# A two-layer decoder trunk on one core: 166 instead of 168 tokens through the first layer's dense experts, and the second layer's mixing tables loaded in that mixing

## The chip, the cores and the metric

The kernel runs on one core of a Trainium2 chip (trn2). The metric is the device time of one execution in microseconds (us); smaller is better. Several executions were timed, and one more was profiled.

## The reference, cut to what matters

Two layers are applied to 256 tokens of 1024 channels. Each layer mixes tokens and then channels:

```python
def hybrid_layer(x, ...):
    h = rms_norm(x, norm1_g) * (1 + sc1) + sh1
    q, k, v, cb, cc, ch, su, sv = split(h @ w_in)
    y_attn = sliding_window_attention(q, k, v, attn_sink, rel_bias)   # needs the bias table
    y_conv = short_conv_mixer(cb, cc, ch, conv_w)
    y_sgu  = chunked_spatial_gating(su, sv, sgu_w, sgu_b)             # needs the gating weights
    x = x + g1 * (concat(rms_norm of the three) @ w_out)
    h2 = rms_norm(x, norm2_g) * (1 + sc2) + sh2
    return x + g2 * peer_ffn(h2, ...)

def peer_ffn(h, w_pq, sub_keys, expert_down, expert_up):
    # per token: 8 heads x 16 experts out of 16384, found by product keys
    act = gelu(einsum('td,thkd->thk', h, expert_down[experts]))
    return einsum('thk,thkd->td', gate * act, expert_up[experts])
```

`expert_down` and `expert_up` have 16384 rows of 1024 floats each in every layer.

## The kernel before

**Stages.** For each of the two layers the program runs `mixing` (attention, convolution and gating, then `w_out`), `retrieval` (which experts each token wants, and with which gate) and `experts`. The last is split into a **down half** (128 steps, one for each group of 128 rows of `expert_down`) and an **up half** (`combine`, 128 steps over `expert_up`).

**Two ways through the experts.** The first `T = DENSE[layer]` tokens go the dense way: TensorE multiplies them with all 16384 experts, 8 matrix products of 128 x 128 by 128 x T for each step in either half, and a gate that is zero for unwanted experts selects. The activations, 128 steps x T columns, lie in the large buffer `arena` (in `acts`); step i of the up half reads the i-th T columns, which are then free. The other `TS = 256 - T` tokens go by rows. They are put in sets of n = 64, 32, 16 or 8 tokens (`token_sets`). For a set of n tokens, each gather (an indirect DMA by POOL, in `fetch`) brings 128 rows of 1024 floats, one to each partition, so that a set takes n gathers from `down_rows` and n from `up_rows`. VectorE (DVE) multiplies a gathered tile with the tokens and sums (`dot`, the down half), or adds it, weighted, to the set's sum (`add_row`, the up half). TensorE adds the set's sum into the result with eight small products, the folds (`fold_set`): `early_folds` puts one behind each of eight steps, starting 8 steps after the set's last row was added; the last set's folds stand in step 127 (`folds`). There are 88 such tokens in the first layer (64 + 16 + 8) and 96 in the second (64 + 32).

**What sets the order.** The engines run their queues in order. The dense weights are streamed in five buffers of 1 MB (`raw`), issued by SP and by ScalarE (ACT) when TensorE has freed one. Gathers are issued by POOL when a buffer for them is free; the buffers are parts of `spots` (the space of `hh`) and of `arena` that are unused just then. Within `experts` and around its ends the program's order is written by hand (`tc.manual_schedule()`, opened by `manual.enter_context` and ended by `manual.close()`). Outside, the order of an engine's queue is chosen at build time by a scheduler that places an instruction where it believes it to be ready.

**The tables.** The mixing needs a bias table (`R_BIAS`, 1 MB), gating weights (`R_SW`, 256 KB) and their offsets (`R_SB`, 128 KB), at columns 45 to 56 x 256 of `arena`. `R_SW` is masked in place by an AFFINE_SELECT on POOL, and two columns of `R_Z` are zeroed. For the second layer the loads are issued on SP's queue in the first layer's up half, in step `56 * S // T + 4`, and the mask follows on POOL in step 124 (`tables_rest`).

Of the kernel before, what the change touches and what calls it, by code (L numbers as in the profile page):

```python
# [18 lines left out]
DEPTH = 2  # L19
S = 256  # L20
DC = 8
# [22 lines left out]
DENSE = (168, 160)  # L44
# [31 lines left out]
def token_sets(n):  # L76

    out, off = [], 0
    for m in (64, 32, 16, 8):
        if n & m:  # L80
            out.append((off, m))
            off += m
    assert off == n and len(out) <= 3
    return out
# [3 lines left out]
def hybrid_trunk(ctx: ExitStack, tc: tile.TileContext, x_in, c_in, vec_in, w_ada, w_first, w_in, w_out, w_pq,  # L88
                 keys, down, down_rows, up, up_rows, rel_bias, sgu_w, sgu_b, out):
    nc = tc.nc  # L90
# [61 lines left out]
    R_HF = region(104 * S, DC, S)  # L152
# [9 lines left out]
    R_BIAS = region(45 * S, 8, S)  # L162
# [404 lines left out]
    def tables(layer, after=None):  # L567
        if after is not None:
            for r in (R_BIAS, R_SW, R_SB):
                nc.scalar.copy(r[:, 0, 0:1], after)  # L570
        q = nc.gpsimd if layer == 0 else nc.sync
        q.dma_start(R_BIAS, rel_bias)
        q.dma_start(R_SW, sgu_w[layer])
        q.dma_start(R_SB, sgu_b[layer])
        return lambda: tables_rest(layer)

    def tables_rest(layer):
        nc.gpsimd.affine_select(R_SW, R_SW, pattern=[[0, 4], [1, P]], compare_op=OP.is_ge, fill=0.0,
                                base=0, channel_multiplier=-1)
        nc.gpsimd.memset(R_Z[:, :, 0:2], 0.0)  # L580
        qg = work.tile([P, 1], F32, name="qg", tag="qg", bufs=1)
        nc.vector.tensor_scalar(qg, vec[:, layer, V_QG:V_QG + 1], 0.125, None, op0=OP.mult)
        return qg
# [8 lines left out]
    def mixing(layer, qg, update=None, late=None):  # L592
# [245 lines left out]
        if layer == 0:  # L838
# [3 lines left out]
            qg = tables(0, R_HF[:, DC - 1, 0:1])()  # L842
            for n, ps in enumerate(pss):
                evac(n, ps)
        else:
# [5 lines left out]
            manual.close()  # L851
            evac(1, ps)
# [202 lines left out]
    def experts(layer, rest):  # L1055
# [4 lines left out]
        NG = T // 4  # L1060
# [5 lines left out]
        R_DROW = spots[:, 3, :]  # L1066
        beyond = [region(at * S, D) for at in (80, 84) if at * S >= P * T]
        passing = []
# [122 lines left out]
        def gate_use(g, ps, done):  # L1191
            v = ps.rearrange("p (t i) -> p i t", t=4)
            a = acts[:, :, 4 * g:4 * g + 4]
# [25 lines left out]
        def combine(layer, late, dotted):  # L1219
# [28 lines left out]
            for i in range(128):  # L1248
# [30 lines left out]
                if i == 56 * S // T + 4 and layer + 1 < DEPTH:  # L1279
                    others = tables(layer + 1)  # L1280
                if i == 124 and layer + 1 < DEPTH:
                    qg = others()
# [18 lines left out]
        for i in range(128):  # L1301
# [8 lines left out]
            if j == 1:  # L1310
                tdone = 4 * gdone
                pend.append((pair, gelu(pair, ps, tdone), tdone))
                if len(pend) > 1:
                    act_use(*pend.popleft())
# [203 lines left out]
```

## Time and profile before

| | us |
|---|---|
| three timed runs | 1544.82, 1545.63 (median), 1546.74 |
| the profiled execution | 1544.97 |
| its span, first to last instruction | 1543.3 |

The table below adds up the busy time of three engines in each stage of the profiled execution, with the share of time in which the 16 DMA engines moved something (by overlapping packets it can pass 1) and what they moved. TensorE's busy time is modelled and counts overlapping products once.

| stage, us from the start | TensorE | VectorE | POOL | DMA share | GB/s |
|---|---|---|---|---|---|
| layer 0 mixing, 0 to 129 | 122.02 | 99.12 | 5.66 | 0.97 | 379 |
| retrieval, 129 to 188 | 58.04 | 48.83 | 5.05 | 0.49 | 171 |
| down half, 188 to 502 | 313.43 | 242.72 | 123.21 | 1.01 | 399 |
| up half, 502 to 800 | 298.00 | 136.80 | 113.46 | 1.01 | 416 |
| layer 1 mixing, 800 to 897 | 96.92 | 64.42 | 0.61 | 0.52 | 174 |
| retrieval, 897 to 955 | 57.04 | 47.84 | 5.06 | 0.49 | 173 |
| down half, 955 to 1255 | 299.27 | 231.75 | 124.94 | 1.00 | 397 |
| up half, 1255 to 1543 | 282.95 | 128.76 | 125.18 | 0.97 | 405 |

### The profile page before, as it was taken

The numbers are of one execution on the slowest core, as the hardware profiler recorded it, in microseconds if no ns is written. First come the engines' busy times: TensorE is split into PE (matmuls) and PEld (weight loads), VectorE is DVE, ScalarE is ACT, GpSimd is POOL, SyncE is SP. The second block draws the span as 40 slices with busy tenths as digits, with TensorE's granted clock in tenths as the row PEclk, the third lists the DMA queues.
The fourth block names the chain that finished last, engine by engine and source line by source line (L and its number), as shares of the span: only waits on it lengthen the run. The fifth ranks groups of instructions, "written<-read, shape, count | busy, mean of one in ns | idle before, by whom it ended". The sixth has DMA issues, their size and how long they took to land.

```text
span 1543.3 us, 28519 instructions
## 1 busy us (share of the span) xinstructions
PE 1527.7 (99%) x11244; PEld 1494.3 (97%) x11244; DVE 1000.2 (65%) x2249; ACT 478.7 (31%) x1380; POOL 503.2 (33%) x424
## 2 busy tenths in 40 slices
PE   8999999999999999999999999999999999999998
PEld 6879999999999999999999899999999999999998
DVE  7787879677687544444467578797777764443435
ACT  2256322466564000000036663234656620000000
POOL 0000125344334433443300002154344444444542
PEclk9999999999999999999999999999999999999999
DMA  9998299999999999999985573999999999999996
GB/s 387 386 362 319 93 312 380 422 422 422 422 422 420 420 422 423 422 424 423 422 319 169 170 257 107 280 409 423 421 423 423 422 422 423 423 423 423 424 422 283
DMA packets 122120, 570.65 MB, mean 370 GB/s; under 512 B 14292, under 2 KB 14820, under 8 KB 89986
## 3 DMA queue, kind: packets, MB, share of 16 engines
q1 hardware_dynamic: 48818, 240.54, 39.7%
q0 software_dynamic: 55744, 202.36, 32.6%
q10 hardware_dynamic: 17424, 125.93, 19.7%
q8 instruction: 88, 1.44, 0.3%
q14 instruction: 46, 0.38, 0.1%
HBM read 563.50 MB, written 4.09 MB: 368 GB/s over the span
## 4 chain that ended last, share of the span: by engine, by line
PE 84%; DMA 10%; DVE 3%; issue 1%; ACT 1%; POOL 0%; DVEq 0%; ACTq 0%; SPq 0%; POOLq 0%
PE acc L1225 37%; PE ch L403 28%; DMA arena<-in_down_rows,arena 5%; DMA spots<-in_down_rows,arena 3%; PE ch L405 2%; PE ch L406 2%; PE ch L407 2%; PE g L1187 2%; PE ch L494 1%; DVE raw L256 1%; PE g L999 1%; PE acc L405 1%; PE acc L407 1%; PE acc L406 1%; DMA raw<-in_w_ada 1%
## 5 line engine op out<-in xcount | busy, mean ns | idle before, releaser
L1225 PE MATMUL acc<-arena,raw 128*128 128x168 f32 (+1 forms) x4096 | 577.0, 303 | 0.0
L1225 PEld LDWEIGHTS acc<-arena,raw 128*128 128x128 f32 x4096 | 570.8, 190 | 0.0
L403 PE MATMUL ch<-arena,raw 128*128 128x168 f32 (+2 forms) x3808 | 564.3, 307 | 0.6 <-issue 0.6
L403 PEld LDWEIGHTS ch<-arena,raw 128*128 128x128 f32 x3808 | 539.3, 190 | 7.6 <-issue 3.9
L1153 DVE SCALAR_TENSOR_TENSOR spots<-arena,spots 128x1024 f32<-128x1024 f32 x154 | 197.8, 1285 | 263.3 <-DMA arena<-in_up_rows,arena 262.0
L1128 POOL DMA_INDIRECT arena<-in_up_rows,arena x159 | 216.6, 1362 | 283.8 <-DMA arena<-in_up_rows,arena 196.8
L1128 POOL DMA_INDIRECT arena<-in_down_rows,arena x147 | 177.0, 1204 | 223.3 <-DVE arena L1138 177.2
L1138 DVE SCALAR_TENSOR_TENSOR arena<-arena,spots 128x1024 f32<-128x1024 f32 x147 | 177.6, 1220 | 47.8 <-DMA arena<-in_down_rows,arena 46.0
L1171 ACT ACTIVATE arena<-arena,parts 128x128 f16<-128x128 f16 x164 | 64.6, 394 | 107.2 <-DVE arena L1161 85.1
L434 ACT ACT_TABLE_LOAD x6 | 7.7, 1283 | 247.9 <-PE acc L1225 247.8
L405 PE MATMUL ch<-hh,hi 128*128 128x256 f32 x288 | 82.6, 289 | 2.0 <-DVE arena L525 1.9
L406 PE MATMUL ch<-hh,lo 128*128 128x256 f32 x288 | 81.8, 284 | 0.0
L407 PE MATMUL ch<-hh,hi 128*128 128x256 f32 x288 | 81.8, 284 | 0.0
L1204 ACT ACTIVATE arena<-ch 128x336 f32<-128x336 f32 (+32 forms) x122 | 42.1, 346 | 123.7 <-PE ch L403 109.5
L1197 DVE SCALAR_TENSOR_TENSOR arena<-arena,g 128x336 f32<-128x336 f32 (+30 forms) x82 | 40.3, 492 | 49.6 <-ACT arena L1195 47.8
L256 DVE SCALAR_TENSOR_TENSOR raw<-raw,arena 128x1024 f32<-128x1024 f32 x48 | 58.4, 1221 | 12.2 <-DMA raw<-in_w_ada 12.1
L1128 POOL DMA_INDIRECT spots<-in_down_rows,arena x37 | 42.1, 1138 | 73.2 <-DVE spots L1138 54.7
L309 DVE TENSOR_TENSOR lo<-raw,hi 128x1024 fp32r<-128x1024 f32 x42 | 51.1, 1224 | 22.1 <-ACT hi L316 19.2
L1175 ACT ACTIVATE arena<-arena,parts 128x128 f16<-128x128 f16 x164 | 63.4, 387 | 0.0
L1173 ACT ACTIVATE arena<-arena,parts 128x128 f16<-128x128 f16 x164 | 63.4, 386 | 0.0
L1177 ACT ACTIVATE arena<-arena,parts 128x128 f16<-128x128 f16 x164 | 63.4, 386 | 0.0
L403 PE MATMUL ch<-arena 128*128 128x168 f32 (+1 forms) x448 | 63.0, 303 | 0.0
(239 smaller groups left out, 1754.9 us busy)
## 6 DMA issues: line engine op xcount, KB each, us to landing
raw<-in_up SPq DMA_DIRECT2D x64, 1024.0 KB
raw<-in_up ACTq DMA_DIRECT2D x64, 1024.0 KB
raw<-in_down SPq DMA_DIRECT2D x58, 1024.0 KB
raw<-in_down ACTq DMA_DIRECT2D x56, 1024.0 KB
raw<-in_w_ada SPq DMA_DIRECT2D x48, 512.0 KB
aside<-in_w_ada SPq DMA_DIRECT2D x48, 512.0 KB
raw<-in_w_pq SPq DMA_DIRECT2D x32, 512.0 KB
arena<-in_down SPq DMA_DIRECT2D x28, 512.0 KB
```

Of the source, the lines that this page charges most:

```text
L256: nc.vector.scalar_tensor_tensor(raw, raw, 1.0, cact, op0=OP.mult, op1=OP.mult, accum_out=mods[layer][:, col:col + 1])
L403: nc.tensor.matmul(dst, hi[:, cols], k[0], start=start, stop=stop, **kw)
L405: nc.tensor.matmul(dst, hi[:, cols], k[0], start=start, stop=False, **kw)
L406: nc.tensor.matmul(dst, lo[:, cols], k[0], start=False, stop=False, **kw)
L407: nc.tensor.matmul(dst, hi[:, cols], k[1], start=False, stop=stop, **kw)
L1128: nc.gpsimd.indirect_dma_start(out=held[n], out_offset=None, in_=rows if n >= TS else down_rows[:, :], in_offset=bass.IndirectOffsetOnAxis ...
L1138: nc.vector.scalar_tensor_tensor(row, row, 1.0, R_DX[which(k)[0]], op0=OP.mult, op1=OP.mult, accum_out=R_DOTS[:, k:k + 1])
L1153: nc.vector.scalar_tensor_tensor(R_SUM[s], row, w, R_SUM[s], op0=OP.mult, op1=OP.add)
L1171: nc.scalar.activation(og[0][:, 0, i, :], oh[:, 0, i, :], AF.Copy, scale=parts[:, 0, t + i:t + i + 1])
L1173: nc.scalar.activation(og[1][:, 0, i, :], oh[:, 0, i, :], AF.Copy, scale=parts[:, 1, t + i:t + i + 1])
L1175: nc.scalar.activation(og[0][:, 1, i, :], oh[:, 1, i, :], AF.Copy, scale=parts[:, 0, t + 2 + i:t + 3 + i])
L1225: nc.tensor.matmul(acc[d // 2][:, (d % 2) * S:(d % 2) * S + T], u[:, d * P:(d + 1) * P], acts[:, i, :], start=i == 0 and d % 2 == 0, stop= ...
```

## The change

The first layer's dense width goes from 168 to 166 tokens. Its rows part grows from 88 to 90 tokens in four sets: 64, 2, 16 and 8. The fourth of the four tiles of `spots` becomes the new set's, and the scratch `R_DROW`, which later serves as a gather buffer, moves to a part of `arena` that was a gather buffer of its own. The gate's one-hot products still run in groups of four tokens; of the last group only two columns are used. The tables of the second layer are now asked for in its own mixing, behind `manual.close()`, on POOL's queue; only the small `qg` product stays in step 124.

```diff
-DENSE = (168, 160)
+DENSE = (166, 160)
...
 def token_sets(n):
-    out, off = [], 0
-    for m in (64, 32, 16, 8):
-        if n & m:
-            out.append((off, m))
-            off += m
-    assert off == n and len(out) <= 3
-    return out
+    sizes = [m for m in (64, 32, 16, 8) if n & m]
+    if n & 2:
+        sizes.insert(1, 2)
+    assert sum(sizes) == n and len(sizes) <= 4
+    return [(sum(sizes[:k]), m) for k, m in enumerate(sizes)]
...
-        q = nc.gpsimd if layer == 0 else nc.sync
-        q.dma_start(R_BIAS, rel_bias)
-        q.dma_start(R_SW, sgu_w[layer])
-        q.dma_start(R_SB, sgu_b[layer])
-        return lambda: tables_rest(layer)
-
-    def tables_rest(layer):
+        nc.gpsimd.dma_start(R_BIAS, rel_bias)
+        nc.gpsimd.dma_start(R_SW, sgu_w[layer])
+        nc.gpsimd.dma_start(R_SB, sgu_b[layer])
         nc.gpsimd.affine_select(R_SW, R_SW, pattern=[[0, 4], [1, P]], compare_op=OP.is_ge, fill=0.0,
                                 base=0, channel_multiplier=-1)
         nc.gpsimd.memset(R_Z[:, :, 0:2], 0.0)
+
+    def q_gain(layer):
         qg = work.tile([P, 1], F32, name="qg", tag="qg", bufs=1)
...
             second_pair(ps)
             first_q(*outputs())
             manual.close()
+            tables(layer)
             evac(1, ps)
...
-        NG = T // 4
+        NG = -(-T // 4)
...
-        R_DROW = spots[:, 3, :]
         beyond = [region(at * S, D) for at in (80, 84) if at * S >= P * T]
+        R_DROW = spots[:, 3, :] if len(SETS) < 4 else beyond.pop()
...
-                if i == 56 * S // T + 4 and layer + 1 < DEPTH:
-                    others = tables(layer + 1)
                 if i == 124 and layer + 1 < DEPTH:
-                    qg = others()
+                    qg = q_gain(layer + 1)
```

Three places show how the instructions stand now. The first is POOL's queue at the end of the first layer's up half and the start of the second layer; `in_up_rows` are gathers (one line is a run of equal ones), `in_keys` belongs to the second layer's mixing. Before:

```order
L1128 DMA arena<-in_up_rows,arena 128x1024 x9
L1128 DMA spots<-in_up_rows,arena 128x1024
L1128 DMA arena<-in_up_rows,arena 128x1024 x2
L578 AFFINE_SELECT arena<-arena 128x512
L580 MEMSET arena 128x2x2
L865 DMA arena<-in_keys 128x2048
```

The same stretch of POOL's queue in the changed kernel, from the first gather of the up half on:

```order
L1126 DMA arena<-in_up_rows,arena 128x1024 x42
L574 MEMSET arena 128x2x2
L1126 DMA arena<-in_up_rows,arena 128x1024 x33
L569 DMA arena<-in_rel_bias 128x2048
L1126 DMA arena<-in_up_rows,arena 128x1024 x3
L570 DMA arena<-in_sgu_w 128x512
L571 DMA arena<-in_sgu_b 128x256
L572 AFFINE_SELECT arena<-arena 128x512
L1126 DMA arena<-in_up_rows,arena 128x1024 x12
L863 DMA arena<-in_keys 128x2048
```

The scheduler has moved the loads, the mask and the MEMSET up, out of the second layer's mixing and in among the first layer's gathers: the three loads stand behind 75 and 78 of the 90 gathers, and 12 gathers stand behind the AFFINE_SELECT, which reads what the load of `in_sgu_w` brings.

The second place is SP's queue in the first layer's up half. Before, the three loads stood between a load for the second layer's modulation (`aside`) and the dense weights (`raw`):

```order
L240 DMA raw<-in_up 128x2048
L242 DMA aside<-in_w_ada 128x1024
L572 DMA arena<-in_rel_bias 128x2048
L573 DMA arena<-in_sgu_w 128x512
L574 DMA arena<-in_sgu_b 128x256
L240 DMA raw<-in_up 128x2048 x3
L1278 DMA arena<-x_dram 128x2048
```

In the changed kernel they are gone from it:

```order
L240 DMA aside<-in_w_ada 128x1024
L238 DMA raw<-in_up 128x2048
L240 DMA aside<-in_w_ada 128x1024
L238 DMA raw<-in_up 128x2048 x3
L1277 DMA arena<-x_dram 128x2048
```

Nothing else moved on SP. The third place is TensorE's queue in the up half, where the folds of the first sets stand. Before, behind 784 products (98 steps):

```order
L1225 MATMUL acc<-arena,raw 128x168 x784
L1233 MATMUL acc<-fold_102,spots 128x64
L1225 MATMUL acc<-arena,raw 128x168 x8
L1233 MATMUL acc<-fold_102,spots 128x64
L1225 MATMUL acc<-arena,raw 128x168 x8
```

In the changed kernel the folds of the set of 64 begin a step earlier, and those of the set of 2 stand beside them:

```order
L1224 MATMUL acc<-arena,raw 128x166 x776
L1232 MATMUL acc<-fold_102,spots 128x64
L1224 MATMUL acc<-arena,raw 128x166 x8
L1232 MATMUL acc<-fold_102,spots 128x64
L1224 MATMUL acc<-arena,raw 128x166 x8
L1232 MATMUL acc<-fold_102,spots 128x64
L1232 MATMUL acc<-fold_102,spots 128x2
```

A fold waits for its set's last row, and the dense products behind it in TensorE's queue wait with it.

More of the change, by code (lines that the diff above doesn't have):

```diff
@@ L841, in mixing @@
             first_chunks(pss, first_norm())
-            qg = tables(0, R_HF[:, DC - 1, 0:1])()
+            tables(0, R_HF[:, DC - 1, 0:1])
+            qg = q_gain(0)
             for n, ps in enumerate(pss):
@@ L1192, in gate_use @@
             v = ps.rearrange("p (t i) -> p i t", t=4)
-            a = acts[:, :, 4 * g:4 * g + 4]
+            a = acts[:, :, 4 * g:min(4 * g + 4, T)]
+            v = v[:, :, :min(4, T - 4 * g)]
             if done < 128:
@@ L1310, in experts @@
             if j == 1:
-                tdone = 4 * gdone
+                tdone = min(4 * gdone, T)
                 pend.append((pair, gelu(pair, ps, tdone), tdone))
```

## The prediction, made before the changed kernel was run

> **What bounds the kernel now.** First the page's head and slices: a single core, whose granted TensorE clock shows no throttle, and a DMA row that stands at 9 wherever the experts run.
>
> ```profile
> span 1543.3 us, 28519 instructions
> PEclk9999999999999999999999999999999999999999
> DMA  9998299999999999999985573999999999999996
> GB/s 387 386 362 319 93 312 380 422 422 422 422 422 420 420 422 423 422 424 423 422 319 169 170 257 107 280 409 423 421 423 423 422 422 423 423 423 423 424 422 283
> ```
>
> The change works in the first layer's experts, so the stage windows come next: the down half once it has started up, and the up half.
>
> ```profile
> 255.00:502.00 247.00, 247.00 (x1920) 245.12 (x1920) 185.34 (x357) 136.09 (x473) 97.93 (x80) 1.00 1.02 422
> 502.00:796.00 294.00, 294.00 (x2073) 294.00 (x2072) 133.50 (x130) 4.80 (x9) 113.46 (x84) 1.00 1.01 419
> ```
>
> The columns are the stretch's length, then TensorE's products and weight loads, VectorE, ACT and POOL, the clock, the DMA share and GB/s. TensorE never idles in either half; the 16 DMA engines do not either, at 419 to 422 GB/s, and no slice of the whole run goes above 424. So **two limits lie on top of each other**. Which of them gives way first is read from the groups of the gather part:
>
> ```profile
> L1153 DVE SCALAR_TENSOR_TENSOR spots<-arena,spots 128x1024 f32<-128x1024 f32 x154 | 197.8, 1285 | 263.3 <-DMA arena<-in_up_rows,arena 262.0
> L1128 POOL DMA_INDIRECT arena<-in_up_rows,arena x159 | 216.6, 1362 | 283.8 <-DMA arena<-in_up_rows,arena 196.8
> L1138 DVE SCALAR_TENSOR_TENSOR arena<-arena,spots 128x1024 f32<-128x1024 f32 x147 | 177.6, 1220 | 47.8 <-DMA arena<-in_down_rows,arena 46.0
> ```
>
> In the up halves VectorE waits 262 us for gathers to land: they take the bandwidth that the dense weights leave. The dense weights come at TensorE's pace, because SP waits for it to free their buffers:
>
> ```profile
> SPq L240 <- PE acc L1225: 483.7, 58, 9.2
> ```
>
> How near the gathers come to holding TensorE up is seen in the timeline, at the last sets' adds on VectorE
>
> ```profile
> 774.99 1.28 DVE L1153 SCALAR_TENSOR_TENSOR spots<-arena,spots 128x1024 f32<-128x1024 f32 x1 [1.46 <-DMA arena<-in_up_rows,arena]
> ...
> 792.24 1.28 DVE L1153 SCALAR_TENSOR_TENSOR spots<-arena,spots 128x1024 f32<-128x1024 f32 x1 [1.18 <-DMA arena<-in_up_rows,arena]
> 794.77 1.28 DVE L1153 SCALAR_TENSOR_TENSOR spots<-arena,spots 128x1024 f32<-128x1024 f32 x1 [1.25 <-DMA arena<-in_up_rows,arena]
> ```
>
> and on TensorE:
>
> ```profile
> 777.80 0.29 PE L1233 MATMUL acc<-fold,spots 128*128 128x16 f32 x2
> ...
> 796.98 0.28 PE L1233 MATMUL acc<-fold,spots 128*128 128x8 f32 x2
> ```
>
> The set of 16 is complete at 774.99 + 1.28 = 776.27 and TensorE folds it at 777.80: 1.5 us to spare. The last row of all is added by 796.05 and folded at 796.98: **0.9 us to spare**. The gathers arrive barely in time, and DMA has nothing left.
>
> **The change part by part.** (1) *Two columns less.* The chain of waits has two long uninterrupted pieces of the up halves, at 168 and at 160 columns:
>
> ```profile
> 502.58 223.44 PE acc L1225 x1568
> ...
> 728.69 2.34 PE acc L1225 x16
> 731.20 2.34 PE acc L1225 x16
> ...
> 1256.27 199.95 PE acc L1225 x1472
> ```
>
> One instruction takes 223.44 / 1568 = 142.5 ns at 168 columns and 199.95 / 1472 = 135.8 ns at 160, so a column costs (142.5 - 135.8) / 8 = 0.83 ns. A half has 128 steps x 8 products x 2 instructions = 2048, so two columns save 2048 x 1.67 ns = 3.4 us in each half, 6.8 us together.
>
> (2) *Eight more folds* for the set of 2. A step with a fold is 731.20 - 728.69 = 2.51 us long, one without 16 x 142.5 ns = 2.28, so a fold costs 0.23 us and eight cost 1.8. TensorE's own balance is -6.8 + 1.8 = **-5.0 us**.
>
> (3) *Four more gathers*, two from `down_rows`, two from `up_rows`: each 128 x 1024 x 4 bytes = 0.524 MB, together 2.10 MB; at 422 GB/s that is **+5.0 us of DMA time**. The tables are still loaded before the last gathers, only on another queue, so that their 1.44 MB neither leave the stage nor come new: 0. What TensorE would gain doesn't count as long as the gathers end later: the fold of the last set then waits for them. The end of the half moves by 5.0 less the 0.9 to spare, **+4.1 us**.
>
> (4) *POOL now waits in the middle of the gathers.* Its DMAs have one queue of their own:
>
> ```profile
> q0 software_dynamic: 55744, 202.36, 32.6%
> ```
>
> 368 gathers of 0.524 MB make 192.9 MB of it. The AFFINE_SELECT waits for `in_sgu_w`, which was issued behind gathers that have not landed, and the last 12 gathers cannot be issued meanwhile. Rows that bear on this, all of POOL:
>
> ```profile
> 39.43 0.58 POOL L573 DMA_DIRECT2D arena<-in_sgu_w  x1
> 48.22 0.63 POOL L578 TENSOR_SCALAR_AFFINE_SELECT arena<-arena 128x512 f32<-128x512 f32 x1 [7.67 <-DMA arena<-in_sgu_w]
> ...
> 230.82 0.61 POOL L1097 DMA_DIRECT2D pair_in<-chosen  x1
> 236.69 2.32 POOL L1102 DMA_DIRECT2D pairs<-pair_in  x4 [5.27 <-DMA pair_in<-chosen]
> ...
> 775.66 1.43 POOL L1128 DMA_INDIRECT arena<-in_up_rows,arena  x1 [1.32 <-DMA arena<-in_up_rows,arena]
> ```
>
> With nothing of POOL's ahead the load took 8.8 us to the select (39.43 to 48.22). Behind gathers, one issued at 775.66 was added at 794.77, 19.1 us later; POOL's wait will be near that. While it lasts the gathers in flight go on landing, so the wait itself costs nothing; the loss is the hole behind it, when `in_sgu_w` has landed and no gather is under way: 0.63 us for the select, 1.43 to issue a gather, and 5.27 until a transfer lands (the row of `pair_in`), less the 794.77 - 792.24 = 2.53 us at which gathers land anyway, 4.8 us. It is nothing if waiting weights fill it wholly, and 7.3 if the pitch isn't credited. I take **4 us**, since the weights' loads that are already under way use some of it.
>
> The Trainium skill, DMA: Bandwidth & Descriptors, section Anatomy of one DMA, fits such a POOL load as 2.0 us plus its bytes at 436 GB/s; for 262144 bytes that is an estimate of 2.6 us. By it POOL would go on before the gathers in flight have run out, the hole would be nothing and the sum 1549.1, the second rival below. The row of 39.43 to 48.22, 8.8 us with DMA busy, speaks against it.
>
> (5) *Small parts.* One gather buffer fewer: 0 to 0.524 MB / 422 GB/s = 1.2 us; I take 0, because POOL mostly waits for landings (196.8 of 283.8 us above), not for buffers. Three more small DMAs of POOL at the start of the down half, 2.32 / 4 = 0.58 us each: 0 to 1.7 us; 0, as the bandwidth there isn't used up (the 282 and 342 below), which hides the 0.5 MB of the new set's inputs too; without that cover they cost 1.2.
>
> ```profile
> 200.00:225.00 25.00, 25.00 (x178) 25.00 (x177) 16.67 (x64) 6.63 (x16) 2.37 (x4) 1.00 1.03 282
> 225.00:250.00 25.00, 25.00 (x178) 25.00 (x177) 24.69 (x136) 3.83 (x12) 15.38 (x17) 1.00 0.94 342
> ```
>
> VectorE's two dots and two adds, 2 x 1.22 + 2 x 1.29 = 5.0 us, lie in its idle time (it is busy 133.5 of 294 us in the up half); they would cost up to that if it were late. SP's queue loses three loads, which frees nothing while its weights wait for TensorE.
>
> Sum, against the profiled execution's own 1544.97 us: 1544.97 + 5.0 - 0.9 + 4.0 = **1553.1 us**. That execution lies 0.7 below the median of the timed runs, within their spread. Its own range goes from 1549.1 (no hole) to 1544.97 + 4.1 + 7.3 + 1.2 + 1.7 = 1559.3.
>
> **The rivals.** *TensorE stays the limit (faster).* If DMA can carry the four gathers in time, for instance because the gathers get ahead where TensorE is held for a moment, TensorE's -5.0 us is the result: 1540.0. For it speaks that no engine waits in the chain, with products and weight loads at 294.00 of 294.00 us. It decides itself at the last add: it would have to end by about 791 instead of 796.05, with 2.1 MB more moved. Against it stand 1.02 and 422 GB/s. The Trainium skill, Perfetto Trace Analysis, section Identifying the Most-Contended Engine, judges TensorE's headroom by the busy share of its weight loads, here 294.00 of 294.00; by that rule alone TensorE is the limit and the time 1540.0. The trace agrees on TensorE, but the row of the gathers shows DMA as full.
>
> *Gathers are late, without a hole.* POOL's wait is short, or the weights fill the gap: 1544.97 + 4.1 = 1549.1; a little less if the weights that TensorE no longer asks for while it waits make room.
>
> *The loads act as the change says.* Were the tables' 1.44 MB really out of the stage, 1.44 / 0.422 = 3.4 us would come off: 1549.1 - 3.4 = 1545.7. The order in the built program speaks against it.
>
> *TensorE stands still over the wait.* The fold of the set of 16 needs four of the 12 gathers behind the select. If POOL is late there, 0.63 + 1.43 + 5.27 + 3 x 2.53 = 14.9 us pass from the landing of `in_sgu_w` until they have landed; if that landing falls where TensorE is already at the fold, with 1.5 us to spare before: 1544.97 + 4.1 + 14.9 - 1.5 = 1562.5.
>
> **How the numbers follow.** Chances: the forecast 0.56, late without a hole 0.18, TensorE the limit 0.14, standing still 0.08, the loads out of the stage 0.04. A measurement of this kernel can tell about 0.2%, 3.1 us: faster is below 1542.5, slower above 1548.7. Faster gets 0.14. The same gets 0.04 and, of the case without a hole, the 0.10 that end below 1548.7: 0.14. Slower gets the rest, 0.72. The range from 1544.5 to 1560 holds the forecast's own, the case without a hole and the loads out of the stage, 0.78, and a little of the standing still.
>
> **What would show it.** In the changed profile: products at about 140.8 ns an instruction in the first layer; on POOL an AFFINE_SELECT with some 20 us of idle time ended by `in_sgu_w`, and behind it a burst of gathers; idle time of TensorE ahead of folds in the first layer's up half, ended by VectorE's adds, with DMA still near 420 GB/s outside the hole; the second layer's stages as long as before. Wrong would be: no idle time ahead of the folds (then DMA had room), a select without a wait (no hole), or stalls in the second layer.

## The result and the profile after

The changed kernel takes **1559.39 us** (median of five runs, 1557.73 to 1562.21) against 1545.63 us (five runs) before: slower by the ratio 1.0090, 95% interval 1.0076 to 1.0104. The profiled execution took 1557.73 us, 12.8 more than that of before. The forecast was 1553.1 in a range of 1544.5 to 1560.0: the direction was right and the time lies at the upper edge of the range, but the time was not lost where the forecast had put it.

The page's head and slices of the changed kernel:

```profile
span 1556.0 us, 28571 instructions
...
PEclk9999999999999999998999999999999999999999
DMA  9998299999999999999985572999999999999996
```

DMA stands where it stood. New is an 8 in the TensorE clock, in the slice from 700 to 739 us. The list of TensorE's waits (us in total, times, longest) names what is new in the first layer's up half; before, no wait of over 0.5 us stood there:

```profile
PE acc L1232 <- DVE spots L1151: 9.6, 1, 9.6
```

One fold (L1232), once, 9.6 us. The timeline of TensorE around it, changed kernel:

```profile
714.74 6.78 PE L1224 MATMUL acc<-arena,raw 128*128 128x166 f32 x47
731.11 0.69 PE L1232 MATMUL acc<-fold,spots 128*128 128x64 f32 x2 [9.59 <-DVE spots L1151]
731.60 4.71 PE L1224 MATMUL acc<-arena,raw 128*128 128x166 f32 x16
736.13 0.34 PE L1232 MATMUL acc<-fold,spots 128*128 128x64 f32 x2
736.31 2.47 PE L1224 MATMUL acc<-arena,raw 128*128 128x166 f32 x16
```

and the same place before:

```profile
717.74 8.29 PE L1225 MATMUL acc<-arena,raw 128*128 128x168 f32 x57
725.86 0.33 PE L1233 MATMUL acc<-fold,spots 128*128 128x64 f32 x2
726.03 2.50 PE L1225 MATMUL acc<-arena,raw 128*128 128x168 f32 x16
```

The fold is the **first of the set of 64**, in the middle of the half, not one of the last sets. VectorE's timeline shows the last row of that set, before:

```profile
719.90 1.28 DVE L1153 SCALAR_TENSOR_TENSOR spots<-arena,spots 128x1024 f32<-128x1024 f32 x1 [1.95 <-DMA arena<-in_up_rows,arena]
721.10 1.22 DVE L256 SCALAR_TENSOR_TENSOR aside<-aside,arena 128x1024 f32<-128x1024 f32 x1
```

and in the changed kernel, where the last three rows stand in one line and the set of 2 begins behind them:

```profile
727.11 3.95 DVE L1151 SCALAR_TENSOR_TENSOR spots<-arena,spots 128x1024 f32<-128x1024 f32 x3 [0.67 <-DMA arena<-in_up_rows,arena]
730.98 0.75 DVE L1149 TENSOR_SCALAR spots<-arena 128x1024 f32<-128x1024 f32 x1
```

Before, the set was complete at 719.90 + 1.28 = 721.18 us and folded at 725.86: 4.7 us to spare. After, it is complete at 731.06, 9.9 us later, and TensorE is there at 714.74 + 6.78 = 721.52, 4.3 us earlier. 9.9 + 4.3 - 4.7 = 9.5 us, the stand.

The stand costs more than its length. The 16 products behind it take 4.71 us instead of 2.47. The table by stretches (columns as in the prediction) shows why:

```profile
721.00:726.00 5.00, 0.52 (x4) 0.27 (x2) 3.27 (x3) 0.00 (x0) 2.74 (x2) 0.99 1.01 417
726.00:736.00 10.00, 4.89 (x18) 4.89 (x19) 8.78 (x11) 0.00 (x0) 6.81 (x7) 0.50 1.02 416
736.00:741.00 5.00, 5.00 (x38) 5.00 (x37) 4.93 (x6) 0.00 (x0) 4.39 (x4) 0.99 1.03 411
```

The granted clock falls to 0.50 some 4.5 us into the stand and stays there until 5 us after it: another 2.2 us. The up half adds up so: -3.4 (narrower products), +1.8 (eight folds), +9.6 (stand), +2.2 (clock) = +10.2 us. Measured from its first products (502.58 before, 502.86 after, in the chain of waits) to its first fold of the last set (796.98 before, 807.82 in the row below), it is 10.56 us longer. The rest of the 12.7 us by which the span grew is 0.3 ahead of the half and some 1.9 behind that fold, and isn't traced further.

What the prediction had put the loss on looks like this in the changed kernel, on POOL, on VectorE and on TensorE:

```profile
742.36 0.60 POOL L570 DMA_DIRECT2D arena<-in_sgu_w  x1
742.93 0.61 POOL L571 DMA_DIRECT2D arena<-in_sgu_b  x1
764.89 0.63 POOL L572 TENSOR_SCALAR_AFFINE_SELECT arena<-arena 128x512 f32<-128x512 f32 x1 [21.36 <-DMA arena<-in_sgu_w]
765.70 1.02 POOL L1126 DMA_INDIRECT arena<-in_up_rows,arena  x1 [0.17 <-issue]
...
762.72 1.28 DVE L1151 SCALAR_TENSOR_TENSOR spots<-arena,spots 128x1024 f32<-128x1024 f32 x1 [0.88 <-DMA arena<-in_up_rows,arena]
770.48 1.28 DVE L1151 SCALAR_TENSOR_TENSOR spots<-arena,spots 128x1024 f32<-128x1024 f32 x1 [6.47 <-DMA arena<-in_up_rows,arena]
...
801.61 1.28 DVE L1151 SCALAR_TENSOR_TENSOR spots<-arena,spots 128x1024 f32<-128x1024 f32 x1 [1.26 <-DMA arena<-in_up_rows,arena]
...
807.82 0.28 PE L1232 MATMUL acc<-fold,spots 128*128 128x8 f32 x2
```

POOL does wait 21.4 us, but all of it after the stand. The hole behind the wait is there too: VectorE waits 6.47 us for the next row, where some 1.2 us are usual, and from 766 to 772 us the loads run at 304 GB/s (420 before). TensorE isn't held by it. The last row is added by 802.89 and folded at 807.82, with 4.9 us to spare instead of 0.9: while TensorE stood, it asked for no weights, and the gathers caught up.

Why are the rows late by 9.9 us? The groups of VectorE from 502 to 721 us show how far it had come, before and after:

```profile
L1153 DVE SCALAR_TENSOR_TENSOR spots<-arena,spots 128x1024 f32<-128x1024 f32 x57 | 73.3, 1285 | 106.8 <-DMA arena<-in_up_rows,arena 105.6 <-DVE spots L1153 1.0
L1153 DVE SCALAR_TENSOR_TENSOR spots<-spots,arena 128x1024 f32<-128x1024 f32 x6 | 7.7, 1284 | 8.4 <-DMA spots<-in_up_rows,arena 8.4
```

```profile
L1151 DVE SCALAR_TENSOR_TENSOR spots<-arena,spots 128x1024 f32<-128x1024 f32 x58 | 74.5, 1284 | 121.2 <-DMA arena<-in_up_rows,arena 121.2
L1136 DVE SCALAR_TENSOR_TENSOR arena<-arena,spots 128x1024 f32<-128x1024 f32 x1 | 1.2, 1224 | 1.7 <-DMA arena<-in_down_rows,arena 1.7
```

With the first row of the set, which is a TENSOR_SCALAR, 64 rows were added before and 59 after, where a dot of the down half stands among them too. VectorE has idle time, ended by landings. So rows are missing, not VectorE's time. Two of the five are the two more gathers of `down_rows`, which stand ahead of all up rows in the queue.

### The profile page after: what moved, and what is told of

The parts are those of the page before. It is cut to its first block, busy times and chain, and to the rows that moved or that the text cites. A ratio compares the mean times of both kernels' runs of the same rounds, so it can differ in the third digit from the quotient of the medians.

```text
span 1556.0 us, 28571 instructions
## 1 busy us (share of the span) xinstructions
PE 1528.1 (98%) x11260; PEld 1491.9 (96%) x11260; DVE 1003.4 (64%) x2257; ACT 475.8 (31%) x1380; POOL 503.2 (32%) x434
## 3 DMA queue, kind: packets, MB, share of 16 engines
q8 instruction: 88, 1.44, 0.3%
## 4 chain that ended last, share of the span: by engine, by line
PE 56%; DMA 26%; DVE 7%; issue 6%; POOL 3%; ACT 2%; ACTq 0%; POOLq 0%; DVEq 0%
PE acc L1224 24%; PE ch L401 15%; DMA arena<-in_up_rows,arena 12%; DMA arena<-in_down_rows,arena 12%; POOL arena L1126 3%; PE ch L403 2%; PE ch L404 2%; PE ch L405 2%; DVE raw L254 1%; PE ch L492 1%; DMA pairs<-chosen 1%; PE g L997 1%; PE g L1185 1%; PE acc L403 1%; PE acc L404 1%
## 5 line engine op out<-in xcount | busy, mean ns | idle before, releaser
L1224 PE MATMUL acc<-arena,raw 128*128 128x166 f32 (+1 forms) x4096 | 576.3, 303 | 0.0
L401 PE MATMUL ch<-arena,raw 128*128 128x166 f32 (+2 forms) x3808 | 561.0, 306 | 0.0
L1151 DVE SCALAR_TENSOR_TENSOR spots<-arena,spots 128x1024 f32<-128x1024 f32 x164 | 210.7, 1285 | 282.0 <-DMA arena<-in_up_rows,arena 281.5
L1126 POOL DMA_INDIRECT arena<-in_up_rows,arena x170 | 227.1, 1336 | 271.0 <-DMA arena<-in_up_rows,arena 195.4
L1126 POOL DMA_INDIRECT arena<-in_down_rows,arena x163 | 192.7, 1182 | 256.8 <-DVE arena L1136 203.0
L1136 DVE SCALAR_TENSOR_TENSOR arena<-arena,spots 128x1024 f32<-128x1024 f32 x163 | 197.4, 1221 | 75.8 <-DMA arena<-in_down_rows,arena 75.5
L1169 ACT ACTIVATE arena<-arena,parts 128x128 f16<-128x128 f16 x164 | 64.6, 394 | 139.9 <-DVE arena L1159 139.9
L1203 ACT ACTIVATE arena<-ch 128x332 f32<-128x332 f32 (+42 forms) x122 | 41.6, 341 | 118.2 <-PE ch L401 114.0
L1171 ACT ACTIVATE arena<-arena,parts 128x128 f16<-128x128 f16 x164 | 63.4, 386 | 0.0
L401 PE MATMUL ch<-arena 128*128 128x166 f32 (+1 forms) x448 | 62.6, 302 | 0.0
L401 PEld LDWEIGHTS ch<-arena 128*128 128x128 f32 x448 | 62.1, 190 | 0.0
## 6 DMA issues: line engine op xcount, KB each, us to landing
aside<-in_w_ada SPq DMA_DIRECT2D x48, 512.0 KB, 12.8
```

The lines of the kernel that those rows point to most:

```text
L401: nc.tensor.matmul(dst, hi[:, cols], k[0], start=start, stop=stop, **kw)
L1126: nc.gpsimd.indirect_dma_start(out=held[n], out_offset=None, in_=rows if n >= TS else down_rows[:, :], in_offset=bass.IndirectOffsetOnAxis ...
L1136: nc.vector.scalar_tensor_tensor(row, row, 1.0, R_DX[which(k)[0]], op0=OP.mult, op1=OP.mult, accum_out=R_DOTS[:, k:k + 1])
L1151: nc.vector.scalar_tensor_tensor(R_SUM[s], row, w, R_SUM[s], op0=OP.mult, op1=OP.add)
L1169: nc.scalar.activation(og[0][:, 0, i, :], oh[:, 0, i, :], AF.Copy, scale=parts[:, 0, t + i:t + i + 1])
L1171: nc.scalar.activation(og[1][:, 0, i, :], oh[:, 0, i, :], AF.Copy, scale=parts[:, 1, t + i:t + i + 1])
```

## The experiments

The table gives, from each profiled execution, where the up half of layer 0 begins, the longest stand of TensorE in it, where layer 1 begins (first product of its first stage) and how long layer 1's mixing takes; and the times with their ratios to the kernel before on the same chip.

| kernel | up half begins | stand | layer 1 begins | its mixing | median us | ratio (95%) |
|---|---|---|---|---|---|---|
| before | 502.4 | none | 799.5 | 96.8 | 1545.63 | |
| changed | 502.7 | 9.6 | 810.6 | 96.8 | 1559.39 | 1.0090 (1.0076 to 1.0104) |
| width_only | 505.1 | 13.0 | 815.7 | 96.8 | 1560.93 | 1.0086 (1.0064 to 1.0107) |
| tables_only | 502.5 | 0.7 | 801.2 | 96.8 | 1547.87 | 1.0001 (0.9985 to 1.0016) |
| late_fold | 503.6 | 13.8 | 818.3 | 99.8 | 1568.61 | 1.0128 (1.0103 to 1.0153) |
| one_buffer_less | 500.8 | 0.6 | 798.8 | 96.8 | 1549.14 | 1.0012 (0.9999 to 1.0026) |
| relief | 504.6 | none | 800.2 | 113.2 | 1564.06 | 1.0106 (1.0089 to 1.0123) |
| relief_168 | 503.4 | 0.5 | 803.2 | 110.9 | 1564.74 | 1.0103 (1.0086 to 1.0120) |
| relief_160 | 495.5 | 10.2 | 790.1 | 116.4 | 1559.85 | 1.0078 (1.0047 to 1.0109) |
| tables_in_mixing | 504.3 | 9.1 | 812.2 | 96.8 | 1558.32 | 1.0066 (1.0048 to 1.0084) |
| thin_asides | 504.8 | 9.4 | 814.5 | 96.8 | 1567.11 | 1.0133 (1.0116 to 1.0150) |
| relief_thin | 506.7 | none | 802.3 | 98.7 | 1549.83 | 1.0016 (1.0004 to 1.0028) |
| asides_up | 497.9 | 4.2 | 834.3 | 96.8 | 1581.60 | 1.0224 (1.0206 to 1.0243) |
| asides_early | 504.8 | none | 800.7 | 96.8 | 1549.38 | 1.0020 (1.0008 to 1.0031) |

The columns in us of stages come from one execution of each kernel. Executions of one kernel differ by some us (the kernel before: 1543.38 to 1553.11 on the first chip), so a difference of a few us between two rows is weak evidence by itself.

The median before was 1547.58 us on the chip of the first four experiments, 1547.87 for the next four, 1546.19 for the three behind them and 1547.39 for the last.

**width_only**: the width and the set of 2 alone; the tables as before, on SP at step 90 of the up half, masked in step 124.

```diff
+        q = nc.gpsimd if layer == 0 else nc.sync
-        nc.gpsimd.dma_start(R_BIAS, rel_bias)
+        q.dma_start(R_BIAS, rel_bias)
...
+                if i == 56 * S // T + 4 and layer + 1 < DEPTH:
+                    others = tables(layer + 1)
```

> The width of 166 with the set of 2, but the tables loaded and masked where they stood before (SP's queue, step 90 of the up half; mask in step 124). Theory bytes (the four more gathers come too late for the first fold of the set of 64, where TensorE stood still for 9.6 us; the tables' move costs nothing): the still-stand stays and is 0 to 3.4 us longer, since the tables' 1.44 MB are now ahead of that fold again: 1557 to 1563 us. Theory tables (POOL's 21.4 us wait for the gating weights makes the gathers late): no still-stand, 1546 to 1550.

The same wait, longer:

```profile
PE acc L1232 <- DVE spots L1151: 13.0, 1, 13.0
```

The tables are here issued at about 705 us, ahead of the stand, and not at 737 us, behind it: 1.44 MB at 422 GB/s are 3.4 us, and the stand is 3.4 us longer, in one execution of each and with an up half that began 2.4 us later. The two ratios don't tell the kernels apart. The whole loss is the width's.

**tables_only**: width 168, the tables as in the changed kernel.

```diff
-DENSE = (166, 160)
+DENSE = (168, 160)
```

> 168 columns as before, but the tables on POOL's queue as in the changed kernel. Theory bytes: TensorE doesn't stand still at the first fold; POOL waits some 20 us for the gating weights, and at most a few us are lost at the last folds: 1545 to 1550. Theory tables: 1554 or more, with TensorE's stand at a fold.

No difference in time: 1.0001, no stand over 0.7 us. POOL waits here too (19.2 us), and the hole follows it (8.72 us without a row for VectorE), but at 168 columns they cost nothing that the times show.

**late_fold**: the changed kernel with the first layer's folds 20 steps behind their set's last row instead of 8.

```diff
-                    d = i - at - FOLD_AFTER
+                    d = i - at - (20 if layer == 0 else FOLD_AFTER)
```

> The changed kernel, but in the first layer a set's folds begin 20 steps after its last row instead of 8, so the first fold stands 12 steps (27 us) later. Theory bytes: the gathers as a whole end too late, so the wait moves to the last folds and keeps most of its size: 1552 to 1558. Theory place (only the early fold of the set of 64 meets late rows, and the gathers catch up by themselves towards the end): TensorE's own -5 us come through in part, 1541 to 1546.

The list of waits shows that the stand moved to the last folds and grew:

```profile
PE acc L1232 <- DVE qg L578: 13.8, 1, 13.8
```

It ends at 810.24 us, and the table by stretches has the clock at half for 14 us more:

```profile
810.00:824.00 14.00, 13.76 (x49) 12.60 (x50) 8.70 (x20) 5.52 (x14) 0.00 (x0) 0.50 0.22 75
```

So a later place for the fold doesn't save the time: TensorE meets late rows at the last folds instead. Not all of the 13.8 us are the bytes, though. POOL's select ran at 780.82 us in this kernel, and VectorE's adds show the hole behind it:

```profile
778.83 1.28 DVE L1151 SCALAR_TENSOR_TENSOR spots<-arena,spots 128x1024 f32<-128x1024 f32 x1 [1.24 <-DMA arena<-in_up_rows,arena]
787.74 1.28 DVE L1151 SCALAR_TENSOR_TENSOR spots<-arena,spots 128x1024 f32<-128x1024 f32 x1 [7.62 <-DMA arena<-in_up_rows,arena]
```

VectorE waits 7.62 us for a row, where it waited 1.24 for the row before. Here the last rows hold TensorE, so an estimated 7.62 - 1.24 = 6.4 us of the stand are the hole that the prediction priced at 4. A late fold without the tables among the gathers was not run, so how far the rows would have caught up by themselves stays open. My 1552 to 1558 us were too low: I had not counted on a longer stand, on the hole or on the clock.

**one_buffer_less**: the kernel before with the tile that the set of 2 takes kept from the gathers in layer 0.

```diff
-                free.append(R_DROW)
+                if layer == 1:
+                    free.append(R_DROW)
```

> The kernel before with one gather buffer fewer in the first layer (the fourth tile of spots is not given to the gathers). Theory bytes: 1545 to 1547. Theory buffer (five instead of six buffers in the down half make the gathers late): 1550 or more, with TensorE held up in the down half or at the first fold.

1.0012, an interval that holds no change, and no stand over 0.6 us: at 168 columns the buffer isn't missed. At 166, where the rows are late, it wasn't tried alone.

**relief**: the changed kernel with 16 loads of `w_ada` (8.4 MB, groups SH2 and SC2 of layer 1) taken out of layer 0's up half and loaded in layer 1's mixing.

```diff
-        body += mix(tail[:6], ada(0, [5])) + tail[6:] if layer == 0 else tail
+        body = body + mix(tail[:6], ada(0, [5])) + tail[6:] if layer == 0 else mix(body + tail, ada(1, [3, 4]), 4, 22)
...
-        aside = ada(1, [0, 1, 2, 3, 4] if layer + 1 < DEPTH else [5], "aside")
+        aside = ada(1, [0, 1, 2] if layer + 1 < DEPTH else [5], "aside")
```

> The changed kernel, with the sixteen loads of w_ada for layer 1's SH2 and SC2 (16 x 0.52 MB = 8.4 MB) taken out of layer 0's up half and put into layer 1's mixing. Theory bytes (TensorE stands at the first folds because the up half's loads are more than its time carries): 8.4 MB at 422 GB/s are 19.9 us of loads, more than the 9.6 us of the stand, so no stand over 1 us is left at the folds, the clock stays at 1.0, layer 1 begins at 797 to 799 us instead of 810.6 and the time is 1542 to 1548 us (two us of it open for the loads' multiplications on VectorE in layer 1's mixing). Rival sets (the set of two itself holds rows up, by its spreads, its folds or its place between the others): the stand stays at 8 to 13 us, layer 1 begins at 808 to 812 and the time is 1556 to 1562 us.

In layer 0 the bytes did what was expected. TensorE comes to the first fold of the set of 64 and doesn't wait:

```profile
723.28 0.33 PE L1232 MATMUL acc<-fold,spots 128*128 128x64 f32 x2
```

There is no stand, and from the start of the up half to layer 1 there are 295.6 us, against 297.1 before less 3.4 plus 1.8 = 295.5. But the time did not fall (1564.06 us, where 1542 to 1548 were expected), because layer 1's mixing grew from 96.8 to 113.2 us. Its stretch, in the kernel before and in this one:

```profile
800.00:897.00 97.00, 96.92 (x752) 90.38 (x752) 64.42 (x128) 61.89 (x132) 0.61 (x1) 1.00 0.52 174
```

```profile
800.00:913.00 113.00, 103.51 (x751) 95.29 (x751) 80.96 (x160) 64.72 (x134) 0.57 (x1) 0.94 0.65 224
```

VectorE's busy time rises by 16.5 us (64.42 to 80.96), TensorE idles 9.5 of 113 us, and its clock falls to 0.94 on average.

**relief_168**: the same edit in the kernel before, as a control.

> The kernel before, with the same sixteen loads moved from layer 0's up half into layer 1's mixing: the control. Theory bytes: at width 168 TensorE was the limit already, with 4.7 us to spare at the first fold and 4.9 at the last, so fewer loads win nothing: layer 1 begins at 799 to 800 us, and the time is that of the kernel before, within 3 us (or up to 3 longer for the multiplications in layer 1's mixing); the relieved kernel at width 166 is 2 to 6 us faster than this one. Rival (the loads were the limit before, too): 5 to 15 us faster than the kernel before.

Its layer 0 wins nothing by the relief (799.5 to 803.2): at 168 columns the loads did not hold TensorE. It is even 3.7 us later, 2.7 of them lost in the up half, and why isn't traced. Its mixing grows likewise. So in layer 0 relief is worth 10.4 us at 166 columns and nothing at 168: the loads became the limit with this change. The expectation missed in the whole time: 1564.74 us is 16.9 above the kernel before, where at most 3 to 6 were expected, and the relieved kernel at 166 columns is 0.7 us faster than this one, within the noise, where 2 to 6 were expected. (The expectation's 4.9 us to spare at the last fold are the changed kernel's; before, they were 0.9.)

**relief_160**: 160 columns in layer 0, 24 loads moved (G1 too).

```diff
-DENSE = (166, 160)
+DENSE = (160, 160)
```

> Width 160 in layer 0 (96 tokens by rows, sets of 64 and 32), with 24 loads of w_ada (G1, SH2, SC2 of layer 1) moved into layer 1's mixing. TensorE: 8 columns less x 0.83 ns x 2048 = 13.6 us in each half, and 8 folds fewer. Loads: 16 gathers more (8.4 MB), 24 loads less (12.6 MB): 4.2 MB less than before, 10 us. Theory bytes: the loads set the end now, so of 27 us on TensorE some 10 + 4.8 to spare come through: about 1531 us, with a range of 1526 to 1545 for stands at the folds and a clock of 0.5 after them; stands of over 3 us are seen at the folds. Rival TensorE (bytes don't bind): 1516 to 1520 us with no stand. Rival sets or order: no faster than before.

Layer 0 ends 9.4 us earlier than before, with a stand of 10.2 us at its last folds, where TensorE alone would have given 27. POOL's select runs at 786.75 us here, behind all gathers and the stand, so no hole is in it: the loads set the end. Layer 1's mixing takes it all back and more (116.4 us). The time expected was wrong by 29 us, since I took the multiplications in layer 1 to be covered.

**tables_in_mixing**: the changed kernel with three one-column copies on ScalarE that keep the tables' loads behind the start of layer 1.

```diff
-            tables(layer)
+            tables(layer, R_HF[:, DC - 1, 0:1])
```

> The changed kernel, with three one-column copies on ScalarE from layer 1's first normalised activations into the tables' places, as layer 0 has them, so that the three loads can't be issued ahead of layer 1's mixing. Theory place (the stand at the first folds at 721 to 731 us comes before the tables, which are issued at 737 us, and TensorE doesn't wait afterwards): nothing changes, the stand is 9 to 13 us, 1556 to 1562 us. Rival total (all loads of the half count, the tables' 1.44 MB too): 3.4 us shorter, 1552 to 1556 us. Rival hole (the wait of POOL's AFFINE_SELECT costs 4 us): 1551 to 1555 us.

The loads now are issued at 816 us, and the stand is 9.1 us as before it. What comes behind the stand doesn't matter to it.

**thin_asides**: the changed kernel with the 40 side multiplications of layer 0's experts on VectorE cut to 8 columns, the loads kept.

```diff
+        m = 8 if layer == 1 and col < G2 else D
-        nc.vector.scalar_tensor_tensor(raw, raw, 1.0, cact, op0=OP.mult, op1=OP.mult,
+        nc.vector.scalar_tensor_tensor(raw[:, :m], raw[:, :m], 1.0, cact[:, :m], op0=OP.mult, op1=OP.mult,
```

> The changed kernel with the 40 side multiplications of layer 0's experts (w_ada of layer 1, groups SH1 to SC2) cut to 8 of their 1024 columns: layer 1's modulation is then not the reference's; every load stays. It takes 40 x about 1.1 us off VectorE, which adds the rows that TensorE stands for, and leaves the loads as they are. Theory bytes: the stand at the first fold of the set of 64 stays at 8 to 13 us, layer 1 begins at 808 to 812 us, 1555 to 1562 us. Rival VectorE (the rows wait for its turn): the stand falls under 4 us, layer 1 begins at 797 to 802, 1543 to 1550 us. The start of the up half: at 502 to 505 us, if loads or ScalarE hold the down half; at 498 to 500, if VectorE's multiplications did.

TensorE's longest wait stays where it was:

```profile
PE acc L1233 <- DVE spots L1152: 9.4, 1, 9.4
```

The stand is 9.4 us with 42 us less on VectorE (6.75 us for these tiles instead of 49.06): it isn't VectorE that makes the rows late. The median came out 5 us above what I expected, which nothing in its profiled execution (span 1558.2 us) explains.

**relief_thin**: relief, with the 16 multiplications in layer 1's mixing cut in the same way.

> The relieved kernel (sixteen loads of w_ada in layer 1's mixing) with those sixteen multiplications cut to 8 of their 1024 columns: layer 1's modulation in its feed-forward half is then not the reference's. Layer 0 as in the relieved kernel, no stand, layer 1 at 799 to 803 us. Theory: the 16 us that layer 1's mixing got longer by (113.2 against 96.8 us) are VectorE's multiplications (16 x 1.2 = 19 us) ahead of work that TensorE waits for, with the clock of 0.5 behind these waits: mixing takes 97 to 101 us, the time is 1543 to 1550 us. Rival (the loads themselves, or the ring that they share with the weights, held the mixing up): mixing stays at 108 to 114 us, 1556 to 1564 us.

Its layer 1's mixing, to compare with the two stretches under relief:

```profile
802.00:901.00 99.00, 97.82 (x755) 90.65 (x755) 66.73 (x161) 61.80 (x132) 0.57 (x1) 1.00 0.73 255
```

Mixing falls from 113.2 to 98.7 us, 1.9 above the kernel before, and the time by 14 us to 1549.83. The loads ran there with little harm (255 GB/s instead of 224); the multiplications were what cost.

**asides_up**: the changed kernel with all 22 side loads of the down half (11.5 MB) put into the up half.

```diff
-ASIDES_AT = ((20,) * 6 + tuple(range(46, 125, 5)), (20,) * 6 + (60, 72))
+ASIDES_AT = ((), (20,) * 6 + (60, 72))
```

> The changed kernel with the 22 side loads (and multiplications) of layer 0's down half moved into its up half: 11.5 MB, 27 us of loads at 422 GB/s, from the one half to the other. Theory bytes: the down half has room, its gathers run ahead as far as the buffers let them, and the up half begins at 498 to 500 us (the 3.4 us of the narrower products that the down half had lost); in the up half the loads are far over what its time carries: the stands at the folds add up to 20 to 35 us, layer 1 begins at 820 to 835 us, 1568 to 1585 us. Rival (the down half is held by ScalarE's gates): the up half begins at 502 to 504 us still. Rival sets: the stand stays at 8 to 13 us.

TensorE's waits in the up half are now for the weights themselves, and for rows:

```profile
PE acc L1224 <- DMA raw<-in_up: 16.2, 12, 3.8
...
PE acc L1232 <- DVE spots L1151: 8.1, 2, 4.2
```

24.3 us together, against 27 us of loads added. At the same time the down half got 4.8 us shorter.

**asides_early**: a gentler use of the same: six side loads more in the down half, at its beginning, where DMA isn't full, and six less in the up half.

```diff
-ASIDES_AT = ((20,) * 6 + tuple(range(46, 125, 5)), (20,) * 6 + (60, 72))
+ASIDES_AT = ((12,) * 6 + (24,) * 6 + tuple(range(46, 125, 5)), (20,) * 6 + (60, 72))
...
-            if start is not None and i % 4 == 3:
+            if i % 4 == 3 if start is not None else layer == 0 and 12 < i < 20:
```

> The changed kernel with six of the side loads of w_ada taken from the end of layer 0's line of 40 to its beginning: six are loaded at step 12 of the down half and multiplied at steps 13 to 19, six more at step 24, so that 28 instead of 22 stand in the down half and 12 instead of 18 in the up half. At 200 to 250 us the loads run at 282 and 342 GB/s, so there is room for 5.5 MB there, against 3.1 MB moved; the up half loses 3.1 MB, 7.5 us of loads. Theory bytes: the stand at the set of 64 falls from 9.6 to 1 to 4 us, layer 1 begins at 798 to 803 us, the time is 1543 to 1550 us: about the kernel before, at best 0.2% below. Rival VectorE (it is busy 24.7 of 25 us at 225 to 250, choosing; six multiplications of 1.2 us ahead of that put the picks off, and with them the gathers): what the up half wins the down half loses, the up half begins 3 to 7 us later, at 506 to 510 us, and the time stays at 1552 to 1562 us. Rival sets: the stand stays at 8 to 13 us.

The first stretch of the down half, 188 to 250 us, in the changed kernel and in this one, and then this one's first fold in the timeline:

```profile
188.00:250.00 62.00, 62.00 (x446) 61.98 (x445) 49.39 (x279) 14.69 (x34) 18.18 (x25) 1.00 0.94 303
```

```profile
188.00:250.00 62.00, 62.00 (x444) 61.90 (x444) 56.35 (x288) 14.59 (x34) 19.91 (x27) 1.00 0.92 328
```

```profile
723.44 0.33 PE L1232 MATMUL acc<-fold,spots 128*128 128x64 f32 x2
```

25 GB/s more in 62 us are 1.6 MB that the up half need not carry, and TensorE folds without a wait. The time is 10 us below the changed kernel's. But it is not below the kernel before (1.0020, 1.0008 to 1.0031): its up half begins 2.4 us later, and wins 1.2. No kernel of this study beats the one before.

## Why the prediction was right, and where not

*Two limits on top of each other, and the loads give way first*: right, and now shown: relief, which takes away loads, takes the stand away at 166 columns and wins nothing at 168; thin_asides, which takes away work of VectorE, doesn't.

*(1) Two columns less, -3.4 us in each half, and (2) eight folds, +1.8*: right in size in the up half. relief's 295.6 us against 295.5 is this sum, and steps with two folds and with one are 2.70 and 2.48 us apart in the changed kernel's chain, 0.22 us for a fold. In the **down half the -3.4 us never came**, and this is the first error: the up half begins at 502.7 instead of 499. What holds the down half is seen in the groups from 262 to 502 us: the dots of rows (L1136, L1138 before) and ScalarE's first scaling of a gate's one-hots (L1169, L1171 before). Before:

```profile
L1138 DVE SCALAR_TENSOR_TENSOR arena<-arena,spots 128x1024 f32<-128x1024 f32 x69 | 83.3, 1219 | 18.2 <-DMA arena<-in_down_rows,arena 17.0 <-issue 1.1
L1171 ACT ACTIVATE arena<-arena,parts 128x128 f16<-128x128 f16 x84 | 33.1, 394 | 49.3 <-DVE arena L1161 35.3 <-DVE arena L1215 8.4 <-issue 4.1
```

Changed, and then TensorE's only wait of size there:

```profile
L1136 DVE SCALAR_TENSOR_TENSOR arena<-arena,spots 128x1024 f32<-128x1024 f32 x86 | 104.0, 1222 | 40.3 <-DMA arena<-in_down_rows,arena 40.1
L1169 ACT ACTIVATE arena<-arena,parts 128x128 f16<-128x128 f16 x84 | 33.1, 394 | 76.6 <-DVE arena L1159 76.6
```

```profile
PE g L1185 <- ACT arena L1169: 1.5, 4, 0.6
```

asides_up:

```profile
L1136 DVE SCALAR_TENSOR_TENSOR arena<-arena,spots 128x1024 f32<-128x1024 f32 x80 | 95.5, 1220 | 15.4 <-DMA arena<-in_down_rows,arena 15.2
L1169 ACT ACTIVATE arena<-arena,parts 128x128 f16<-128x128 f16 x84 | 33.1, 394 | 37.5 <-DVE arena L1159 37.5
```

VectorE's dots wait 40 us for rows instead of 17, the one-hots behind them in its queue come later, ScalarE waits for these, and at times TensorE for ScalarE. That list of waits holds 1.5 us only, where 3.7 are missing (502.7 against 499.0); where the rest goes isn't shown. Of the dots 86 fall into this stretch, 69 before: the gathers were behind from the beginning. With the side loads out of the way the dots' wait is 15 us and the up half begins at 497.9. With the multiplications alone cut it begins at 504.8, so VectorE's time isn't it. All kernels at 166 columns with their side loads in place begin it at 502.7 to 506.7, those at 168 at 500.8 to 503.4.

*(3) The gathers' 5.0 us less the 0.9 to spare, at the last fold*: **this is the step that failed**. The term +4.1 stands for a stand of 9.6 us and 2.2 of half clock. I read the slack at the last two sets, where it was least (0.9 and 1.5 us), and not at the set of 64, whose first fold had 4.7 us. But the set of 64 comes first, its fold moves a step ahead, TensorE gets there 4.3 us earlier, and its last row comes 9.9 us later, not the 2.5 us of the two gathers of `down_rows` that stand ahead of it. The byte sum was applied to the end of the half, as if rows and weights were served evenly up to there. Measured against the profiled execution of before, the change cost 0.3 us ahead of the up half, 10.6 in it and 1.9 behind it; the forecast had +4.1 and, for term (4), +4.0. Which part of the 9.9 us is the late start of the gathers and which the weights that TensorE asks for sooner, the runs don't separate.

*(4) The hole behind POOL's wait, 4 us*: right as a hole, wrong as a cost of this kernel. The wait was there, 21.4 us, where some 19 were expected, and the gathers came in a burst. The hole was there too: 6.47 us without a row, 5.2 more than the usual 1.2, where 4.8 had been worked out. But after the stand the rows had 4.9 us to spare at the end, hole included, so TensorE never met it. From the start of the up half to layer 1 the changed kernel and tables_in_mixing, whose gathers have no such wait among them, both take 307.9 us; tables_only (1.0001) shows no cost at 168 columns. (The ratios 1.0090 and 1.0066 alone would not exclude a cost of 4 us.) Only in late_fold, where the last rows hold TensorE, does the hole count. That the forecast's sum came near was luck: +4 for a hole that cost nothing here stood in for a part of a stand that wasn't counted.

One reading behind this term was wrong. The row of 39.43 to 48.22 us was taken as a load with nothing of POOL's ahead, but POOL had issued the 1 MB of the bias table just before it, at 38.70 us. By the fit in the Trainium skill, DMA: Bandwidth & Descriptors, section Anatomy of one DMA, the estimate for such a load was 2.6 us. It doesn't carry over to a queue with work ahead: 21.4 us here.

*(5) The small parts, 0*: held for the buffer at 168 columns (one_buffer_less, 1.0012) and for VectorE (thin_asides). POOL's three small DMAs were not tried by themselves.

*The rivals*: TensorE as the limit did not come true, since no kernel with 166 columns and all its loads in place ran without a stand. Standing still (1562.5) had the right kind of event, but for this kernel the wrong place and cause: at the set of 16, by POOL's wait. That the tables don't leave the stage was right of the built program; were they really out (tables_in_mixing), nothing would have been won, because they are asked for behind the stand.

## What to carry to other kernels

Where TensorE and the loads are both full, work taken from the one must be matched by bytes taken from the other, and the place to look is not the end of the stage but every point where TensorE waits for a sum: write down the slack at each, and move both its sides. Count for a stand its length and the slow clock behind it. Bytes are best moved to a stretch where DMA has room *and* the engine that must work on them has room: six loads moved to the beginning of the down half were worth 10 us, while 16 moved to layer 1's mixing won 10 us in layer 0 and cost 16 there.

## What the hardware showed beyond that

The granted clock falls to 0.50 within a stand and stays there behind it: around the stand of 9.6 us for 10 us in all, around width_only's 13.0 for some 14. Behind late_fold's 13.8 us it came back only after 14 us, though the trace has TensorE busy in 13.76 of these 14.00 us (row above). The first 8 of them are mostly folds of 8 and 16 columns, and the wide products behind them began at 818.33 us, 5.7 us before the clock was back; whether narrow products count for the clock wasn't tried. The Trainium skill, TensorE: Matmul & The Clock Gate, section Part 1: The HAM clock gate, says that the clock halves after an idle window of about 3.4 us and is restored after a busy one. The changed kernel's stand agrees (half from 4.5 us into it until 5 us behind it); late_fold's 14 us don't, if busy means what the profile calls busy.

Short waits were followed by the slow clock too. In the down half of width_only TensorE waited for two gates and then ran at half clock, though it idled for only some 2 us:

```profile
307.41 0.52 PE L1185 MATMUL g<-arena 128*128 128x128 f16 x2 [1.41 <-DVE arena L1159]
308.58 1.11 PE L1185 MATMUL g<-arena 128*128 128x128 f16 x6 [0.65 <-ACT arena L1169]
...
311.00:313.00 2.00, 2.00 (x9) 2.00 (x8) 2.00 (x4) 1.44 (x5) 0.42 (x2) 0.50 1.02 424
```

From 300 to 320 us its mean clock is 0.91. The same 0.91 stands there in tables_in_mixing, thin_asides, relief_thin and asides_early, and 1.00 in the changed kernel and in the kernels at 168 columns. Those five begin the up half at 504.3 to 506.7 us, 1.6 to 4.0 later than the changed kernel. The slow clock, 0.09 of 20 us or 1.8, can be a part of that, but relief begins at 504.6 without it.
